# Splitting weights into two parts ahead of their phase and keeping the parts in DRAM

## The chip, the core and the metric

The kernel runs on one core of a Trainium2 chip. The metric is device microseconds of one execution. The engines are named as in the profile: PE (TensorE, with PEld for its weight loads), DVE (VectorE), ACT (ScalarE), POOL (GpSimd) and SP (SyncE, which here only issues DMAs). Each engine works through its own instructions strictly in order; semaphores order the engines against each other. A DMA issued on an engine stands in that engine's order, so an issue that must wait holds up whatever is behind it.

## The reference

Two transformer blocks run one after the other on 2048 tokens of width 1024, all in float32. Cut to what matters:

```
# block 1: gated linear attention (GLA), 4 heads, chunks of 64 tokens
h = rmsnorm(x, g) * (1 + scale) + shift
q, k, v, g_lr, r = split(h @ w_in)
o = chunked_gla(q, k, v, log_sigmoid(g_lr @ w_alpha + b) / 16)
x = rmsnorm(x + gate * ((rmsnorm(o) * silu(r)) @ w_out), final_g)
# block 2: three mixers side by side on one projection
h2 = rmsnorm(x, g_pre) * (1 + scale2) + shift2
p = h2 @ w_in2
y_m = mlstm(p) * silu(mz)            # 4 heads of 96, chunks of 64
y_a = sliding_window(p) * silu(az)   # "swa": 6 heads, 2 kv heads, window 128
y_s = stick_breaking(p) * silu(sz)   # "stick": 4 heads of 64
out = x + gate2 * rmsnorm(concat(y_m, y_a, y_s) @ w_out2, g_post)
```

## The kernel before, in words

**Tiles and phases.** Tokens go in 8 tiles of 256. Six phases follow one another: the GLA phase (two passes over the 8 tiles, head pair p=0 and then p=1, so 16 tiles), out1 (the output projection of block 1, weights `w_out1`), swa (`d_w`), mlstm (`e_wv`, `e_w`), stick (`c_w`) and out2 (`w_out2`). Intermediate tensors (`hT`, `oT`, `h2T`, `yT`) lie in DRAM.

**Precision.** A float32 operand is used as a high part rounded to fp32r and a low part, the rest. `dense3_steps` makes each dense product from three matmuls, high by high (L280), low by high (L281) and high by low (L282). So every weight must be split once.

**Weights.** A phase holds four weight units, `u0` to `u3` (GLA also `wr0`, `wr1`), each as a high and a low tile of [128, 8, 256] (`u0h`, `u0l`), with one buffer per name. A unit of the next phase may therefore be written only after the last matmul of this phase that reads the old one. `weights` (L153) fetches a unit in pieces of 128x512 floats (256 KB) into tiles called `stage`, of which two exist, and splits each piece as it comes: odd pieces with a Copy on ACT (L174) and a subtraction on POOL (L175), even pieces with a scaling on POOL (L150) and a subtraction on DVE (L151). The DMAs are issued on SP (L168).

**Order.** `pipeline` (L180) runs the tiles of a phase. While tile t is mixed (attention or recurrence), `interleave` (L27) takes in turns steps of that mix and steps of the gate of tile t and the dense products of tile t+1. In the last tile of a phase the loads and splits of the next phase's units are emitted there. The emitted program then goes through a scheduler that orders the instructions of each engine by a simulated timeline and by priorities (`high_priority` in `ahead`). So the final order on an engine isn't the emitted one, and it is fixed when the program is built.

**Names used below.** `la`, `E`, `sil`, `vh`, `osq` belong to a GLA tile (`la` is written once per tile on ACT, L584; `bm` on POOL, L592; `vh` on ACT, L549; S0/S1 are the state). `vf` (ACT, L998) is written once per swa tile; L1103 is swa's division of probabilities on POOL. `hn` (POOL, L1396), `nu`, `wsR`, `lfR`, `rows` and `bc` belong to mlstm: gates are written to `rows` in DRAM (L1154, L1160) and read back broadcast as `bc` (L1269), both on SP. `xr` (L786) is the normalised output of block 1, which PE transposes (L364). `ke`, `be`, `aT`, `po` belong to stick.

Of the kernel before, what the change touches and what calls it, by code (L numbers as in the profile page):

```python
# [21 lines left out]
NT = S // T  # L22
# [1 line left out]
EPS = 1e-6  # L24


def interleave(a, na, b, nb):  # L27

    ia = ib = 0
    while a is not None or b is not None:  # L30
        if b is None or (a is not None and ia * nb <= ib * na):
            if next(a, StopIteration) is StopIteration:
                a = None
            ia += 1
        else:
            if next(b, StopIteration) is StopIteration:
                b = None
            ib += 1


class Bank:
# [27 lines left out]
class K:  # L69

    def __init__(self, tc, I, O, ctx):
        self.tc, self.nc, self.I, self.O, self.ctx = tc, tc.nc, I, O, ctx
        nc = self.nc
        P = self.pool
        self.cp = P("cp", 1)
        self.sp = P("stage", 2)
        self.dp = P("dp", 1, DRAM)
        self.wp = P("w", 1)
        self.hp = P("h", 4)
        self.mmp = P("ps_mm", 2, PSUM)  # L80
        self.nmm = self.nw = 0
# [24 lines left out]
        self.acts = []  # L106
        self.table("natural_log_exp_and_others")
# [45 lines left out]
    def weights(self, src, name, stage=None, pool=None, k0=0, k1=None, more=None):  # L153


        pool = pool or self.wp
        k1, n = k1 or src.shape[1], src.shape[2]
        rows = 2 if n == 256 else 1
        w = n + (more.shape[2] if more is not None else 0)
        hi = pool.tile([128, k1 - k0, w], F32R, name=name + "h", tag=name + "h", bufs=1)  # L160
        lo = pool.tile([128, k1 - k0, w], F32R, name=name + "l", tag=name + "l", bufs=1)
        parts = [(src, 0, n, j, min(j + rows, k1)) for j in range(k0, k1, rows)]
        if more is not None:
            parts.insert(1, (more, n, w, k0, k1))
        for d, c0, c1, j, je in parts:
            shape = [128, je - j, c1 - c0]
            st = stage(shape) if stage else self.sp.tile(shape, F32, name="stage", tag="stage")
# [12 lines left out]
    def pipeline(self, n, load, dense, nd, gate, ng, mix, nm, first, lead=0, nxt=None, pri=0):  # L180

        hs = {0: first[0]}
        out, n0 = [], 0
        if first[1]:
            hs[1] = load(1)
        for i, _ in enumerate(first[1] or dense(0, hs[0])):
            if i == 6 and 1 not in hs:  # L190
                hs[1] = load(1)
        if nxt:
            hload, units, ndense, n0 = nxt

        def both(t):
            W = []
            if t + 1 == n and nxt:
                out.append(hload())
                W += [u() for u in units[:2]]
            yield from gate(t, hs.pop(t))  # L200
            if t + 2 < n:
                with self.tc.high_priority(offset=-30):
                    hs[t + 2] = load(t + 2)
            if t + 1 < n:
                yield from dense(t + 1, hs[t + 1])
            elif nxt:
                W += [u() for u in units[2:]]
                out.append(W)
                out.append(ndense and ndense(0, out[0], W))
                if n0:  # L210
                    yield from islice(out[2], n0)
        for t in range(n):
            gt = ng(t) if callable(ng) else ng
            b, nb, na = both(t), gt + (nd if t + 1 < n else n0), nm(t)
            if not nb:
                list(b)
            for _ in range(gt if t < lead else 0):
                next(b)
            interleave(self.ahead(mix(t), pri), na if nb >= 2 * gt else na // 2, b, nb)
        return out  # L220

    def ahead(self, steps, n):
# [215 lines left out]
    def gla_pass(self):  # L438
        nc, tc, I = self.nc, self.tc, self.I
        gw = I["gla_w"]  # L440
        names = ["u0", "u1", "u2", "u3", "wr0", "wr1"]
        W, ST, st = {}, [None, None], {}

        def unit(p, i, **kw):
            return self.weights(I["gla_wr"][p, i - 4] if i > 3 else gw[p, i], names[i], pool=wr if i > 3 else None,
                                more=None if i else I["gla_wx"], **kw)

        def h_of_x(t, parts):
            for k, h in parts:
                nc.sync.dma_start(self.hT[t][:, k:k + 2, :], h)  # L450
                yield k, h

        with ExitStack() as ctx:
            self.psum(ctx, "gla", mm=2, tr=1, pA=1, po=1, kv=1)
            wr = self.open(ctx, "w_gla", 1)
# [12 lines left out]
            parts = self.make_h(wk, banks, self.G1, None, (("hn", 2), ("hn", 2), ("vh", 3), ("vh", 3)))  # L468
            h0 = self.split_h(h_of_x(0, parts), self.B1)
# [26 lines left out]
            def mix(t):  # L496
# [3 lines left out]
                if 6 < t < 15:  # L500
                    self.late_mod(wk, t - 7)

            return self.pipeline(2 * NT, load, dense, 8, gate, 4, mix, lambda t: 6, (h0, None), pri=100,
                                 nxt=(lambda: self.split_h(self.load_h(self.oT[0], wk, 2, 2, "hn")),
                                      self.units("w_out1"), None, 0))

# [227 lines left out]
    def units(self, key):  # L734

        n = self.I[key].shape[0]
        return [lambda j=j: self.weights(self.I[key][j], f"u{j + 4 - n}") for j in range(n)]

    def halves(self, W):

# [281 lines left out]
    def swa_pass(self, h0, W, first):  # L1022
        nc, I = self.nc, self.I
        with self.swa_ctx as ctx:
# [40 lines left out]
            nxt = self.units("e_w")  # L1065
            nxt.insert(0, self.mlstm_wv)
            self.nxt = self.pipeline(NT, lambda t: self.load_hl(self.h2T[t]), lambda t, h: self.swa_dense(t, h, W), 5,
                                     gate, 3, mix, lambda t: 18, (h0, first), pri=60,
                                     nxt=(lambda: self.load_hl(self.h2T[0]), nxt, self.mlstm_dense, 5))

    def swa_rows(self, wk, n, i, qs, kst, v, bias, sink, y, st):
# [99 lines left out]
    def mlstm_open(self):  # L1171
# [11 lines left out]
        m["hg"], m["sk"] = const("m_hg", [128, 3]), const("m_sk", [128, 3])  # L1183
        for key in ("wq", "wk"):
            m[key] = [one(f"{key}{x}", [128, 6, 96], F32R) for x in "hl"]
            for i in range(2):
                js = slice(3 * i, 3 * i + 3)
                st = self.sp.tile([128, 3, 96], F32, name="stage", tag="stage")
# [6 lines left out]
        m["st"], m["ub"] = {}, {}  # L1195

    def mlstm_wv(self):
        parts = [self.weights(self.I["e_wv"], name, None, pool, k0, k1)
                 for name, pool, k0, k1 in (("u0", None, 0, 5), ("ux", self.m_w1, 5, NK))]
        return [a + b for a, b in zip(*parts)]  # L1200

# [353 lines left out]
```

## Time and profile before

| what | before |
|---|---|
| runs | 2162.48, 2162.74, 2167.41 us; median 2162.74 |
| profiled execution | 2172.11 us; span 2170.4 us |
| granted clock over the span | 0.983 of full speed |
| busy PE / DVE / ACT / POOL | 95% / 62% / 41% / 40% |
| moved over the span | 240.01 MB, 111 GB/s |
| q1 (hardware queue, mostly SP's issues) | 187.17 MB, 28.1% of 16 engines |

The span is the profiled execution from its first to its last instruction. PE is busy for 95% of it, so whatever shortens the time without taking matmuls away must come from the other 5%, about 108 us, or from stretches at a lower clock. The 40 slices of the page show PE at 9 in nearly all slices, with dips at the start and at the borders between phases.

### The profile page before, as it was taken

To read this page: it belongs to the slowest core of one execution; us is meant where nothing else is said; L and a number is where in the kernel's file an instruction comes from. 1 tells how busy PE (TensorE), PEld (TensorE's weight loads), DVE (VectorE), ACT (ScalarE), POOL (GpSimd) and SP (SyncE) were. 2 spreads that over 40 slices of the span, in tenths; PEclk is the share of its full clock that TensorE was granted. 3 is DMA by queue.
4 is the path that set the end of the run, shared out by engine and by line. 5 is a ranking of instruction groups with operands and counts; after the bars stand their busy time and mean duration, and the time that the engine had idled before them with its cause. 6 is when DMAs were issued, how large, how long until landed. Compare 5 with 4: busy or idle time off the path is not lost.

```text
span 2170.4 us, 39224 instructions
## 1 busy us (share of the span) xinstructions
PE 2062.5 (95%) x14912; PEld 1880.4 (87%) x14912; DVE 1354.9 (62%) x2517; ACT 894.8 (41%) x2290; POOL 868.6 (40%) x1362
## 2 busy tenths in 40 slices
PE   6999999899999999979999989999789999889998
PEld 6899999899999878879999889999789998777787
DVE  6755655665666467656555545556447788888843
ACT  3534433333333333345555433533335555544411
POOL 3522334522222356554333423334336555663300
PEclk9999999999999999999999999999989999999999
DMA  9522322432332366663222542333431111222252
GB/s 323 181 78 69 107 83 80 138 101 74 88 86 80 118 232 231 212 223 99 93 93 80 153 83 68 90 107 96 115 115 45 45 45 45 65 68 74 67 186 88
DMA packets 122413, 240.01 MB, mean 111 GB/s; under 512 B 13248, under 2 KB 39782, under 8 KB 122224
## 3 DMA queue, kind: packets, MB, share of 16 engines
q1 hardware_dynamic: 108400, 187.17, 28.1%
q0 software_dynamic: 13824, 50.34, 7.3%
q8 instruction: 117, 1.92, 0.4%
q14 instruction: 72, 0.59, 0.1%
HBM read 178.66 MB, written 58.79 MB: 109 GB/s over the span
## 4 chain that ended last, share of the span: by engine, by line
PE 72%; DMA 8%; POOL 6%; DVE 6%; issue 5%; ACT 2%; SPq 0%; DVEq 0%; POOLq 0%; ACTq 0%
PE mm L280 18%; PE mm L282 18%; PE mm L281 18%; PE po L49 3%; PE aT L951 2%; PE qk L1308 1%; PE z L833 1%; DMA stage<-in_c_w 1%; PE z L834 1%; DVE ke L941 1%; DMA stage<-in_w_out 1%; DMA stage<-in_ada_w 1%; PE pT L1112 1%; DMA bc<-rows 1%; POOL u2l L175 1%
## 5 line engine op out<-in xcount | busy, mean ns | idle before, releaser
L941 DVE TENSOR_TENSOR_SCAN ke<-ke,zero 128x512 f32<-128x512 f32 (+3 forms) x160 | 179.6, 1137 | 19.9 <-POOL ke L936 11.5
L280 PE MATMUL mm<-hh,u1h 128*128 128x256 f32 x640 | 187.1, 292 | 1.3 <-DVE mz L976 1.3
L282 PE MATMUL mm<-hh,u1l 128*128 128x256 f32 x640 | 185.5, 290 | 0.0
L281 PE MATMUL mm<-hl,u1h 128*128 128x256 f32 x640 | 184.9, 289 | 0.0
L280 PE MATMUL mm<-u0h,hh 128*128 128x272 f32 (+2 forms) x464 | 155.2, 334 | 12.8 <-DVE y L1437 4.1
L282 PE MATMUL mm<-u0h,hl 128*128 128x272 f32 (+2 forms) x464 | 154.2, 333 | 0.7 <-DVE hl L265 0.4
L281 PE MATMUL mm<-u0l,hh 128*128 128x272 f32 (+2 forms) x464 | 154.0, 332 | 0.0
L280 PE MATMUL mm<-hh,u2h 128*128 128x256 f32 x512 | 147.6, 288 | 1.1 <-DVE gs L568 1.0
L282 PE MATMUL mm<-hh,u2l 128*128 128x256 f32 x512 | 147.1, 288 | 0.0
L281 PE MATMUL mm<-hl,u2h 128*128 128x256 f32 x512 | 146.4, 286 | 0.0
L280 PEld LDWEIGHTS mm<-hh,u1h 128*128 128x128 f32 x640 | 123.8, 193 | 2.3 <-DVE mz L976 1.5
L280 PE MATMUL mm<-u3h,hh 128*128 128x256 f32 (+1 forms) x384 | 124.3, 324 | 0.9 <-DVE vl L550 0.8
L282 PEld LDWEIGHTS mm<-hh,u1l 128*128 128x128 f32 x640 | 123.8, 193 | 0.6 <-issue 0.2
L281 PEld LDWEIGHTS mm<-hl,u1h 128*128 128x128 f32 x640 | 123.7, 193 | 0.5
L282 PE MATMUL mm<-u3h,hl 128*128 128x256 f32 (+1 forms) x384 | 123.3, 321 | 0.0
L281 PE MATMUL mm<-u3l,hh 128*128 128x256 f32 (+1 forms) x384 | 122.5, 319 | 0.0
L280 PE MATMUL mm<-hh,u3h 128*128 128x256 f32 x384 | 111.5, 290 | 4.6 <-ACT sv L864 2.7
L137 ACT ACTIVATE be<-z 128x512 f32<-128x512 f32 (+3 forms) x160 | 86.6, 541 | 69.2 <-PE aT L951 69.0
L282 PE MATMUL mm<-hh,u3l 128*128 128x256 f32 x384 | 111.1, 289 | 0.2 <-DVE mprev L1194 0.2
L281 PE MATMUL mm<-hl,u3h 128*128 128x256 f32 x384 | 111.2, 290 | 0.0
L280 PEld LDWEIGHTS mm<-u0h,hh 128*128 128x128 f32 x464 | 89.1, 192 | 20.7 <-DVE y L1437 4.8
L137 ACT ACTIVATE ke<-z 128x512 f32<-128x512 f32 (+3 forms) x160 | 86.5, 543 | 47.1 <-PE z L834 17.6
(419 smaller groups left out, 6933.8 us busy)
## 6 DMA issues: line engine op xcount, KB each, us to landing
hh<-h2Th POOLq DMA_DIRECT2D x48, 512.0 KB, 6.7
hl<-h2Tl POOLq DMA_DIRECT2D x48, 512.0 KB, 5.8
mvw<-in_mod_w SPq DMA_DIRECT2D x48, 256.0 KB
stage<-in_ada_w SPq DMA_DIRECT2D x32, 256.0 KB
xt<-in_x SPq DMA_DIRECT2D x16, 512.0 KB
stage<-in_gla_w SPq DMA_DIRECT2D x32, 256.0 KB
oT<-oT SPq DMA_DIRECT2D x32, 256.0 KB
hf<-hT SPq DMA_DIRECT2D x32, 256.0 KB
```

The source lines that it names most:

```text
L49: i = self.k.nc.tensor.matmul(out, a, b, start=first is None, stop=stop, skip_group_check=True).ins
L137: i = self.nc.scalar.activation(out, src, func, **kw).ins
L175: self.nc.gpsimd.tensor_tensor(y, st, x.bitcast(F32), op=OP.subtract)
L280: mm(out, ah[k][:, ca], bh[k][:, cb], start=(k == 0), stop=False)
L281: mm(out, ah[k][:, ca], bl[k][:, cb], start=False, stop=False)
L282: mm(out, al[k][:, ca], bh[k][:, cb], start=False, stop=(k == NK - 1))
L833: mm(out, qs[:, h, qt], ks, start=True, stop=False)
L834: mm(out, qs[:, 2 + h, qt], ks, start=False, stop=True)
L941: nc.vector.tensor_tensor_scan(ke[:, 0:w][:, ::-1], ke[:, 0:w][:, ::-1], zero.to_broadcast([128, w]), ke[:, w:w + 1], op0=OP.mult, op1=OP.add)
L951: nc.tensor.transpose(pa[:, j, :], be[:, j * 128:(j + 1) * 128], self.ident)
L1112: nc.tensor.transpose(pt[:, g, :], ss[g][:, kv, sb * 128:(sb + 1) * 128], self.ident)
L1308: mm(p[:, hh, :], w[a][:, idx, :], cu[b][:, blk, :], start=n == 0, stop=n == len(blocks) - 1)
```

## The change

Weights of the first GLA pass are loaded and split as before. All other weights (217 pieces of 128x256 floats, 128 KB, or slightly smaller) go through a generator, `presplit`: a piece is loaded into a tile `wst` (SP, L208), its high part is written into `wsh` by a Copy on ACT (L214) and stored to a DRAM tensor `wd_...h` (SP, L215); the low part is made in place in `wst` by a subtraction on POOL (L216) and stored to `wd_...l` (SP, L217). `wst` and `wsh` have two buffers each. `interleave` calls `tick` after each step, and from the 25th call on each second call emits one step of the generator: in the GLA phase and in the swa phase only. In the GLA phase the loads are ordered behind the last store of `hT` emitted so far (`anchor`), which exists only in the first pass. At the change of phase `ready` loads a unit's parts in four DMAs of 512 KB; nothing is split there any more. `m_wq` and `m_wk` use the same `wst` tiles, in three steps of two heads' columns.

```
+    def presplit(self):
...
+        for p in pieces + [None]:
+            if p:
+                st = self.sp.tile(list(p[0].shape), F32R, name="wst", tag="wst")
+                i = nc.sync.dma_start(st.bitcast(F32), p[0]).ins
+                if self.anchor:
+                    self.behind(i, self.anchor)
+            if old:
+                ot, dst = old
+                hi = self.sp.tile(list(ot.shape), F32R, name="wsh", tag="wsh")
+                nc.scalar.activation(hi, ot.bitcast(F32), AF.Copy)
+                nc.sync.dma_start(dst[0], hi.bitcast(F32))
+                nc.gpsimd.tensor_tensor(ot, ot.bitcast(F32), hi.bitcast(F32), op=OP.subtract)
+                nc.sync.dma_start(dst[1], ot.bitcast(F32))
+            old = p and (st, p[1])
+            yield
+
+    def tick(self):
+        self.nticks += 1
+        if self.nticks > 24 and self.nticks % 2 == 0:
+            next(self.pre, None)
+
+    def ready(self, key, name, pool=None, k0=0, k1=None):
...
+        for a, b in ((k0, m), (m, k1)):
+            for w, d in zip(tiles, self.wd[key]):
+                self.nc.sync.dma_start(w[:, a - k0:b - k0, :].bitcast(F32), d[:, a:b, :].bitcast(F32))
...
-            interleave(self.ahead(mix(t), pri), na if nb >= 2 * gt else na // 2, b, nb)
+            interleave(self.ahead(mix(t), pri), na if nb >= 2 * gt else na // 2, b, nb, self.tick if ticks else lambda: None)
...
         def unit(p, i, **kw):
+            if p:
+                return self.ready(("gla", i), names[i], wr if i > 3 else None)
...
-                nc.sync.dma_start(self.hT[t][:, k:k + 2, :], h)
+                self.anchor = nc.sync.dma_start(self.hT[t][:, k:k + 2, :], h).ins
...
-        return [lambda j=j: self.weights(self.I[key][j], f"u{j + 4 - n}") for j in range(n)]
+        return [lambda j=j: self.ready((key, j), f"u{j + 4 - n}") for j in range(n)]
...
-        parts = [self.weights(self.I["e_wv"], name, None, pool, k0, k1)
+        parts = [self.ready(("e_wv", 0), name, pool, k0, k1)
```

Three places show what the scheduler made of it. The first is ACT in the fourth GLA tile of the second pass, from `la` on (the first row is once per tile). Before:

```order
L584 ACTIVATE la<-mm 128x512
L722 ACTIVATE oT<-tr,gg 128x2x128 x2
L137 ACTIVATE la<-la 128x512
L137 ACTIVATE la<-la,ones 128x512
L137 ACTIVATE eb<-b 128x512
L137 ACTIVATE E_6128<-bm 128x512
L137 ACTIVATE bm<-bm 128x512
L137 ACTIVATE dl<-dl 128x512
L549 ACTIVATE vh<-mm 128x256
L681 ACTIVATE kTh<-tr 128x512
L549 ACTIVATE vh<-mm 128x256
L137 ACTIVATE sil<-mm 128x512
```

Now, in the same tile:

```order
L646 ACTIVATE la<-mm 128x512
L214 ACTIVATE wsh<-wst 128x256
L784 ACTIVATE oT<-tr,gg 128x2x128 x2
L139 ACTIVATE la<-la 128x512
L214 ACTIVATE wsh<-wst 128x256
L139 ACTIVATE la<-la,ones 128x512
L139 ACTIVATE eb<-b 128x512
L214 ACTIVATE wsh<-wst 128x256
L139 ACTIVATE E_6750<-bm 128x512
L214 ACTIVATE wsh<-wst 128x256
L139 ACTIVATE bm<-bm 128x512
L139 ACTIVATE dl<-dl 128x512
```

Copies of pieces (`wsh<-wst`) stand between the instructions of the tile, five of them in these rows. Between this `la` and the next there are 16 of them; in the six tiles t = 3 to 8 there are 10, 9, 12, 10, 12 and 6, and in t = 9 to 13, where no `hT` store holds them back, 13, 15, 16, 17 and 15.

The second place is SP in the swa phase, with the stores of swa's result (`yT<-ya`) of tiles 2 to 6. Before, the stores follow one another until the next phase's weights are fetched:

```order
L1062 DMA yT_106<-ya 128x768
L1062 DMA yT_107<-ya 128x768
L1062 DMA yT_108<-ya 128x768
L1062 DMA yT_109<-ya 128x768
L168 DMA stage<-in_e_wv 128x392 x6
L168 DMA stage<-in_e_w 128x512 x4
L1062 DMA yT_110<-ya 128x768
```

Now, from the store of tile 2 on (the others are apart in the same way):

```order
L1124 DMA yT_106<-ya 128x768
L208 DMA wst<-in_c_w 128x256 x2
L215 DMA wd_c_w1h<-wsh 128x256 x2
L217 DMA wd_c_w1l<-wst 128x256 x2
L208 DMA wst<-in_c_w 128x256 x2
L215 DMA wd_c_w1h<-wsh 128x256 x2
L217 DMA wd_c_w1l<-wst 128x256 x2
L208 DMA wst<-in_c_w 128x256 x2
L215 DMA wd_c_w2h<-wsh 128x256 x2
L217 DMA wd_c_w2l<-wst 128x256 x2
L208 DMA wst<-in_c_w 128x256 x2
L215 DMA wd_c_w2h<-wsh 128x256 x2
```

The pieces go in pairs: two loads, two stores of the high part, two of the low part. A later load, and a result's store, stand behind the pair's stores, which wait for ACT and POOL. Per swa tile 4, 9, 11, 10, 9 and 10 pieces stand there, and 20 more at the end of the phase and beside the first mlstm tile.

The third place is SP at the change from mlstm to stick, where `rows` and `bc` are mlstm's own. Before:

```order
L168 DMA stage<-in_c_w 128x512 x2
L1333 DMA yT_109<-ym 128x768
L168 DMA stage<-in_c_w 128x512 x4
L1154 DMA rows<-lfR 4x256
L1269 DMA bc_17061<-rows 128x4x256
L168 DMA stage<-in_c_w 128x512
L1160 DMA rows<-lfR 4x256
L168 DMA stage<-in_c_w 128x512
L1269 DMA bc_17063<-rows 128x4x256
L168 DMA stage<-in_c_w 128x512 x6
```

Now:

```order
L236 DMA u1h<-wd_c_w1h 128x1024
L236 DMA u1l<-wd_c_w1l 128x1024
L236 DMA u1h<-wd_c_w1h 128x1024
L236 DMA u1l<-wd_c_w1l 128x1024
L1216 DMA rows<-lfR 4x256
L1331 DMA bc_18408<-rows 128x4x256
L236 DMA u2h<-wd_c_w2h 128x1024
L1222 DMA rows<-lfR 4x256
L236 DMA u2l<-wd_c_w2l 128x1024
L236 DMA u2h<-wd_c_w2h 128x1024
L236 DMA u2l<-wd_c_w2l 128x1024
L1331 DMA bc_18410<-rows 128x4x256
```

The pieces through `stage`, whose buffers come free as ACT, POOL and DVE split them, are replaced by loads into the unit itself, and the two `bc` of this place stand behind such loads instead of behind `stage`. On ACT, POOL and DVE the splits of these units are gone from this place.

## Rows read from the trace of the kernel before

**Rows 1.** The page, part 1: PE's busy time.

```profile
PE 2062.5 (95%) x14912; PEld 1880.4 (87%) x14912; DVE 1354.9 (62%) x2517; ACT 894.8 (41%) x2290; POOL 868.6 (40%) x1362
```

**Rows 2.** Windows: stretch, its length, busy by engine, granted clock, DMA share, GB/s.

```profile
350.00:430.00 80.00, 72.90 (x538) 66.85 (x537) 45.48 (x83) 28.20 (x66) 40.87 (x51) 0.98 0.43 129
445.00:715.00 270.00, 270.00 (x2036) 252.50 (x2035) 163.09 (x321) 91.08 (x213) 72.67 (x117) 1.00 0.29 85
720.00:780.00 60.00, 55.06 (x279) 44.21 (x278) 29.85 (x44) 19.38 (x48) 28.24 (x37) 1.00 0.51 170
920.00:980.00 60.00, 49.14 (x339) 46.14 (x338) 34.73 (x55) 23.27 (x54) 34.43 (x55) 0.91 0.66 212
985.00:1180.00 195.00, 195.00 (x1585) 181.92 (x1585) 116.73 (x266) 109.06 (x338) 72.23 (x118) 1.00 0.27 89
1185.00:1300.00 115.00, 102.11 (x717) 95.59 (x716) 58.75 (x123) 48.73 (x138) 39.02 (x53) 0.94 0.46 115
1500.00:1600.00 100.00, 79.43 (x616) 77.08 (x614) 47.87 (x94) 34.43 (x109) 42.50 (x60) 0.88 0.41 120
1860.00:1940.00 80.00, 69.78 (x528) 59.31 (x527) 68.62 (x96) 40.54 (x90) 58.66 (x86) 0.96 0.23 68
```

**Rows 3.** PE's waits, 350 to 450 us: line, releaser, us, times, longest.

```profile
PE tr L719 <- DVE sil L714: 1.6, 1, 1.6
```

**Rows 4.** PE's waits, 720 to 790 us.

```profile
PE po L664 <- POOL S1h L150: 1.6, 1, 1.6
```

**Rows 5.** PE's waits, 920 to 985 us.

```profile
PE tr L364 <- DVE xr L786: 8.6, 1, 8.6
PE mm L280 <- POOL u3h L150: 1.9, 1, 1.9
```

**Rows 6.** DVE's timeline near 944 us: start, us, instruction, idle before and releaser.

```profile
943.77 1.74 DVE L151 TENSOR_TENSOR u1l<-stage,u1h 128x512 fp32r<-128x512 f32 x1 [1.45 <-POOL u1h L150]
945.44 2.46 DVE L786 TENSOR_SCALAR xr<-x,sm 128x1024 f32<-128x1024 f32 x1
```

**Rows 7.** PE's waits, 1500 to 1610 us.

```profile
PE tr L1401 <- POOL hn L1396: 9.8, 2, 5.3
PE nu L1363 <- DVE w L1356: 2.9, 2, 2.1
PE mm L280 <- ACT sv L864: 2.7, 1, 2.7
```

**Rows 8.** ACT's timeline, 1524 to 1531 us.

```profile
1530.82 0.63 ACT L174 ACTIVATE u2h<-stage 128x512 fp32r<-128x512 f32 x1 [6.39 <-DMA stage<-in_c_w]
1531.36 0.19 ACT L137 ACTIVATE sm<-sm 128x4 f32<-128x4 f32 x1
```

**Rows 9.** PE's waits, 1850 to 1945 us.

```profile
PE po L49 <- DVE aT L955: 5.9, 5, 2.5
```

**Rows 10.** Timelines of SP and POOL: issue and first use of one 256 KB load.

```profile
357.84 1.53 SPq L168 DMA_DIRECT2D stage<-in_gla_w  x2
...
360.88 0.62 POOL L150 TENSOR_SCALAR u0h<-stage 128x512 fp32r<-128x512 f32 x1 [1.87 <-DMA stage<-in_gla_w]
```

**Rows 11.** Chain of waits: one store of 4 KB, one of 256 KB.

```profile
1519.54 1.24 DMA rows<-lfR
...
2060.59 2.41 DMA out<-y
```

**Rows 12.** Instructions by line: count, ns min/median/max, first and last start, forms.

```profile
L175 POOL TENSOR_TENSOR u1l<-stage,u1h x14: 1260/1288/2489, 47.8 to 1890.2; 128x512 fp32r<-128x512 f32 x14
...
L998 ACT ACTIVATE vf<-mm x6: 383/384/384, 1012.8 to 1172.5; 128x256 f32<-128x256 f32 x6
...
L1103 POOL TENSOR_TENSOR s<-s,den x42: 609/1040/1054, 995.5 to 1174.4; 128x512 f32<-128x512 f32 x39, 128x256 f32<-128x256 f32 x3
...
L151 DVE TENSOR_TENSOR u1l<-stage,u1h x14: 660/694/1770, 43.8 to 1893.0; 128x512 fp32r<-128x512 f32 x14
```

**Rows 13.** L592, once per GLA tile, between 445 and 725 us.

```profile
L592 POOL TENSOR_TENSOR bm<-b x7: 1061/1062/1066, 456.5 to 717.7; 128x512 f32<-128x512 f32 x7
```

More of the change, by code (lines that the diff above doesn't have):

```diff
@@ L24, with interleave @@
 EPS = 1e-6
-def interleave(a, na, b, nb):
+def interleave(a, na, b, nb, tick):
     ia = ib = 0
@@ L38, in interleave @@
             ib += 1
+        tick()
 class Bank:
@@ L80, in __init__ @@
         self.mmp = P("ps_mm", 2, PSUM)
-        self.nmm = self.nw = 0
+        self.nmm = self.nw = self.nticks = 0
+        self.wd, self.pre, self.anchor = {}, self.presplit(), None
         self.fence = None
@@ L166, in weights @@
             shape = [128, je - j, c1 - c0]
-            st = stage(shape) if stage else self.sp.tile(shape, F32, name="stage", tag="stage")
+            st = stage(shape)
             i = self.nc.sync.dma_start(st, d[:, j:je, :]).ins
@@ L178, in weights @@
         return [hi[:, k, :] for k in range(k1 - k0)], [lo[:, k, :] for k in range(k1 - k0)]
-    def pipeline(self, n, load, dense, nd, gate, ng, mix, nm, first, lead=0, nxt=None, pri=0):
+    def presplit(self):
+        nc, I = self.nc, self.I
+        jobs = [(("gla", i), [(I["gla_w"][1, i], 0)] + ([(I["gla_wx"], 256)] if i == 0 else [])) for i in range(4)]
+        jobs += [(("gla", 4 + i), [(I["gla_wr"][1, i], 0)]) for i in range(2)]
+        jobs += [(("w_out1", i), [(I["w_out1"][i], 0)]) for i in range(4)]
+        jobs += [(("d_w", i), [(I["d_w"][i], 0)]) for i in range(4)]
+        jobs += [(("e_wv", 0), [(I["e_wv"], 0)])] + [(("e_w", i), [(I["e_w"][i], 0)]) for i in range(3)]
+        jobs += [(("c_w", i), [(I["c_w"][i], 0)]) for i in range(4)]
+        jobs += [(("w_out2", i), [(I["w_out2"][i], 0)]) for i in range(4)]
+        pieces = []
+        for key, parts in jobs:
+            K_, w = parts[0][0].shape[1], parts[-1][1] + parts[-1][0].shape[2]
+            d = self.wd[key] = [self.dp.tile([128, K_, w], F32R, name=f"wd_{key[0]}{key[1]}{x}") for x in "hl"]
+            for src, c0 in parts:
+                n = src.shape[2]
+                rows = max(1, min(K_, 256 // n))
+                cols = n // -(-n // 256)
+                for k in range(0, K_, rows):
+                    for c in range(0, n, cols):
+                        ks, cs = slice(k, k + rows), slice(c0 + c, c0 + c + cols)
+                        pieces.append((src[:, ks, c:c + cols], [x[:, ks, cs].bitcast(F32) for x in d]))
+        old = None
+        for p in pieces + [None]:
[13 more added lines that the diff above has]
+            yield
@@ new lines, in tick @@
+    def tick(self):
[3 more added lines that the diff above has]
+    def ready(self, key, name, pool=None, k0=0, k1=None):
+        pool = pool or self.wp
+        out = []
+        k1 = k1 or self.wd[key][0].shape[1]
+        m = (k0 + k1) // 2
+        tiles = [pool.tile([128, k1 - k0, d.shape[2]], F32R, name=name + x, tag=name + x, bufs=1)
+                 for x, d in zip("hl", self.wd[key])]
+        for a, b in ((k0, m), (m, k1)):
+            for w, d in zip(tiles, self.wd[key]):
+                self.nc.sync.dma_start(w[:, a - k0:b - k0, :].bitcast(F32), d[:, a:b, :].bitcast(F32))
+        return [[w[:, k, :] for k in range(k1 - k0)] for w in tiles]
@@ L185, in pipeline @@
+    def pipeline(self, n, load, dense, nd, gate, ng, mix, nm, first, lead=0, nxt=None, pri=0, ticks=False):
         hs = {0: first[0]}
@@ L501, in mix @@
                     self.late_mod(wk, t - 7)
-            return self.pipeline(2 * NT, load, dense, 8, gate, 4, mix, lambda t: 6, (h0, None), pri=100,
+            return self.pipeline(2 * NT, load, dense, 8, gate, 4, mix, lambda t: 6, (h0, None), pri=100, ticks=True,
                                  nxt=(lambda: self.split_h(self.load_h(self.oT[0], wk, 2, 2, "hn")),
@@ L1067, in swa_pass @@
             self.nxt = self.pipeline(NT, lambda t: self.load_hl(self.h2T[t]), lambda t, h: self.swa_dense(t, h, W), 5,
-                                     gate, 3, mix, lambda t: 18, (h0, first), pri=60,
+                                     gate, 3, mix, lambda t: 18, (h0, first), pri=60, ticks=True,
                                      nxt=(lambda: self.load_hl(self.h2T[0]), nxt, self.mlstm_dense, 5))
@@ L1185, in mlstm_open @@
             m[key] = [one(f"{key}{x}", [128, 6, 96], F32R) for x in "hl"]
-            for i in range(2):
-                js = slice(3 * i, 3 * i + 3)
-                st = self.sp.tile([128, 3, 96], F32, name="stage", tag="stage")
+            for i in range(0, 6, 2):
+                js = slice(i, i + 2)
+                st = self.sp.tile([128, 2, 96], F32R, name="wst", tag="wst").bitcast(F32)
                 nc.sync.dma_start(st, I["m_" + key][:, js, :])
```

## The prediction

> **What bounds the kernel now.** I read the page's first part, then a table of windows, then PE's waits in the windows where PE isn't full, then the timelines of the engines that PE waited for there. PE is busy for 2062.5 us of a span of 2170.4 [rows 1], so some 108 us are idle. The windows show where: in the steady GLA tiles (445 to 715 us) and in the steady swa tiles (985 to 1180) PE is busy for the whole stretch at clock 1.00, while around each change of phase it loses time [rows 2]: 7.1 us at the change of GLA pass (350 to 430), 4.9 before out1 (720 to 780), 10.9 before swa (920 to 980), 12.9 before mlstm (1185 to 1300), 20.6 before stick (1500 to 1600) and 10.2 before out2 (1860 to 1940). These 66.6 us are all that the change can win, plus the stretches where the granted clock was below full: .91 before swa, .88 before stick [rows 2]. What it adds, it adds where PE has no idle time at all.
>
> The waits name what PE lost there. At 350 to 450 it is seven waits of 0.3 to 1.6 us on products of DVE, POOL and ACT, the longest for `sil` [rows 3], spread over engines that split weights. Before out1 it waited 1.6 us for POOL's `S1h` [rows 4]. Before swa one wait of 8.6 us was for `xr` of DVE, and one of 1.9 for a split weight [rows 5]; DVE's timeline shows why: a weight subtraction (`u1l`, 1.74 us) that waited for POOL's half stood ahead of `xr`, which itself took 2.46 [rows 6]. Before stick PE waited 9.8 us for `hn`, in two waits of 5.3 and 4.5 us, then 2.9 and 2.7 us for `nu` and `sv` [rows 7]. The first has a plain cause: ACT sat idle for 6.39 us with a Copy of `u2h` whose `stage` piece was late, and the `sm` that `hn` needs stood right behind it [rows 8]. Before out2 PE waits for DVE's `aT` [rows 9] in a window where DVE is busy for 68.62 of 80 us, POOL for 58.66 [rows 2], both with splits among it.
>
> **What goes.** After the first GLA pass no split stands at a border, so I take the waits above that have a split ahead of them. Change of GLA pass: all 7.1, say 7. Out1: 3.0 of the 4.9 (the `S1h` wait of 1.6, the rest splits of the same units; out1's own first tile keeps the other 1.9). Swa: of 8.6 + 1.9 I keep 3.7, because the new order puts the transposes of `xr` behind 44 dense matmuls where 57 stood before, so `xr` still ends last; gain 6.8, and some 2 more if the clock of .91 rises with the gaps gone: 9. Stick: the first `hn` wait of 5.3 goes, and 5.2 of small waits, together 10.5; 2.5 for the clock (79.43 us of matmuls at .88; full clock would give back 9.5, and I take a quarter since half the gaps stay): 13. The second `hn` wait (4.5), `nu` and `sv` are in mlstm's own recurrence and stay. Out2: 8 of 10.2, since 16 pieces' splits go from a window in which POOL and DVE are the wait: half of them cost POOL 1.29 each, half cost POOL .62 and DVE .69 [rows 10, 12], 15 us of POOL and 5.5 of DVE. Sum of gains: 7 + 3 + 9 + 13 + 8 = 40 us. Bounds: 20 (half of each, where another late engine takes a wait's place) to 66.6 plus about 9 for clock.
>
> What is late next at a border is the weight itself: 2 MB a unit instead of 1. The DMA share there is .41 to .66 [rows 2] with 1 MB units; doubling the weights' part leaves room, and each unit waits for its last reader in any case. I cost it at nothing, with 0 to 10 as bounds. SP issues 652 more DMAs; two issues took 1.53 us with their waits [rows 10], and nearly all the new ones stand in stretches where SP has little else, so they count only within the round below. The smaller loads of `m_wq` and `m_wk` lie beside swa and cost nothing; uncovered they would be six DMAs in place of four, some 3 us.
>
> **What is added in the steady tiles.** 217 pieces, each with a load, a Copy on ACT, a subtraction on POOL and two stores. Durations: ACT .38 us by the Copy of the same shape (`vf`) [rows 12]; POOL .65, half of 1.29 for twice the width [rows 12]. 217 of them are 83 us on ACT and 141 on POOL, in stretches where ACT is busy for 34 to 56% and POOL for 27 to 37% [rows 2]. That fits by busy time. What need not fit is the order. Two `wst` and two `wsh` buffers mean that a pair of pieces must be loaded, copied, subtracted and stored before the next pair's load may write; and since SP, ACT and POOL run their instructions in the built order, a late piece holds up the tile's own `la`, `bm` and `hf` loads behind it. So a tile takes at least (pieces / 2) x P, with P the time of one pair's round.
>
> P from rows: a 256 KB load took 3.04 us from issue to first use [rows 10], a 4 KB store 1.24 and a 256 KB store 2.41 [rows 11]. Half way between, 128 KB load in 2.1 and store in 1.8. 2.1 + .38 + .65 + 1.8 = 4.9; .3 for semaphores and SP's issue makes 5.2. To this .3 because POOL's subtraction reached 2.49 us where it met others (median 1.29) [rows 12], and .4 for pieces that arrive while ACT or POOL is in an instruction of its own (.5 to 1 us). P = 5.9 us. Bounds: 3.8 with both DMAs near the 4 KB row, 7.5 with both at the 256 KB rows and the same .7 on top.
>
> A GLA tile takes 43.5 us (six steps from 456.5 to 717.7) [rows 13]; a swa tile 31.9 (five steps from 1012.8 to 1172.5) [rows 12]. In GLA tiles 3 to 8 there are at most 12 pieces: 6 x 5.9 = 35.4, they fit. In tiles 9 to 13 there are 13, 15, 16, 17 and 15: at 5.9 the last four need 44.3, 47.2, 50.2 and 44.3, an excess of .8 + 3.7 + 6.7 + .8 = 12 us. At P = 5.1 it is nothing, at 6.2 21, at 6.7 37, at 7.5 68. In swa, with at most 11 pieces, it is 1 at 5.9, 8 at 6.7, 24 at 7.5. Beside this single pieces delay swa's chain, where POOL's division of 1.04 us [rows 12] feeds the transposes: of 53 pieces one in five with its .65 us unhidden is 7 us (bounds 0 and 34, all of them). Before mlstm, where the last 20 pieces, 8 MB of ready weights and mlstm's first `rows` and `bc` share SP, I take +4 on top of the waits there (bounds 0 and 10).
>
> The Trainium skill, "DMA: Bandwidth & Descriptors", section "Anatomy of one DMA — SWDGE (gpsimd) path", puts a DMA at about 2.0 us fixed and the rest by bytes; I estimate from it 2.3 us for 128 KB, for a load as for a store. By it P would be .7 longer, 6.6, the GLA excess some 34 us instead of 12 and the sum about +12, rival (a) below. The 4 KB store in 1.24 us speaks for a smaller fixed part [rows 11], so I stay at the rows' value.
>
> POOL and DVE collide as well: DVE's `u1l` subtraction ranged from 660 to 1770 ns [rows 12]. The Trainium skill, "SBUF — State Buffer", tells of a shared port pair that GpSimd and VectorE lock against each other, so that the second waits. The ranges agree; it is in the .3 above, and by a full lock each piece would delay DVE by up to .65 us, which DVE's idle 40% takes in GLA [rows 2].
>
> **The sum.** -40 + 12 + 1 + 7 + 4 = -16 us. From the profiled execution's 2172.1 us that is 2156. That execution is 9.4 us over the median of the runs, 2162.74; the same difference from the median gives 2147 us.
>
> **Rivals.** (a) The pair's round throttles. With P at 6.4 or more, the excess in GLA tiles 9 to 13 and in swa eats the gain: at 6.7 it is 37 + 8 + 7 + 4 - 40 = +16, at 7.5 it is 68 + 24 + 7 + 4 - 40 = +63, so 2179 to 2226 us. For it: PE has no slack in these stretches, four tiles stand over the limit at 5.9 already, and a pair's order leaves two buffers no room. Against: the DMAs have .27 to .29 of their share in use there [rows 2], and 4 KB in 1.24 us. It decides from P = 6.4 on, where the sum is zero. Chance .30.
>
> (b) Nothing much. The waits at the borders are taken by what was second there (`nu`, `sv`, `xr`, late 2 MB units), so the gain is 20 instead of 40, against the same 24 of additions: +4; with gain 25 it is -1. 2157 to 2168 us. For it: small waits of several engines in the first window, and the order of the transposes in out1's end. Against: the 6.39 us of ACT [rows 8], whose cause is removed. Chance .14.
>
> (c) The round fits. P at 5.1 or less: -40 + 0 + 0 + 3 + 0 = -37, and with the clock back to 1.00 in the windows before swa and stick up to 8 more: 2118 to 2126. For it: the busy shares; against: queueing behind the tile's own instructions. Chance .16.
>
> My forecast, a gain of 8 to 30 us (2133 to 2155), has .40.
>
> **How the numbers follow.** A measurement of this kernel can't tell less than about .3%, 6.5 us, from no change. Faster: the forecast's .40 and (c)'s .16, .56. Same: (b), .14. Slower: (a), .30. The range: 2118 takes in (c); at the top I go into (a) up to P of about 7, 2195, beyond which about .1 is left. The forecast's own range is 2133 to 2155.
>
> **What would show it.** Right: no weight splits at the borders from 350 us on, the ACT gap before `sm` gone, and PE's waits at 350 to 430 and before out2 under 3 us each. In GLA's second pass, PE waits of some 12 us in all, with ACT, POOL or SP waiting for `wst` loads or stores, and tiles 9 to 13 longer than 43.5 us; in swa short waits for `s` or `pT`. Wrong: tiles 9 to 13 at 50 us or more (then (a)), or at 43.5 with no waits (then (c)), or border waits of the old length under other names (then (b)).

## The result, and the profile after

The changed kernel takes 2286.75 us (median of 4 runs, 2283.67 to 2289.78) against 2165.07 for the kernel before: a ratio of 1.0559 (95% interval 1.0543 to 1.0574). It is 122 us slower; 16 us faster was forecast. The profiled execution took 2289.44 us, 117.3 more than before's.

The page of the kernel after, part 1 and two groups of part 5 (busy us, mean ns, then the idle time before them and what ended most of it); the first line answers to [rows 1]:

```profile
PE 2103.0 (92%) x14912; PEld 1912.5 (84%) x14912; DVE 1295.4 (57%) x2464; ACT 933.7 (41%) x2453; POOL 920.2 (40%) x1472
...
L216 POOL TENSOR_TENSOR wst<-wst,wsh 128x256 fp32r<-128x256 f32 (+2 forms) x217 | 159.6, 741 | 375.2 <-ACT wsh L214 338.5
L214 ACT ACTIVATE wsh<-wst 128x256 fp32r<-128x256 f32 (+2 forms) x217 | 88.3, 411 | 415.3 <-DMA wst<-in_w_out 99.1
```

The pieces' work is small (88 us on ACT, 160 on POOL), but ACT stood idle for 415 us with a Copy next in its order, and POOL for 375 with a subtraction next. Not all of that is loss, since both engines also had idle time before the change.

Windows of the kernel after, in the order and with the columns of [rows 2], each moved to the same place in the program:

```profile
394.00:474.00 80.00, 74.43 (x527) 68.37 (x526) 35.87 (x70) 30.14 (x75) 27.12 (x43) 0.96 0.83 275
495.00:770.00 275.00, 235.12 (x1610) 215.58 (x1609) 130.94 (x262) 93.51 (x242) 108.09 (x166) 0.93 0.55 165
820.00:880.00 60.00, 58.67 (x321) 49.47 (x321) 26.05 (x39) 16.27 (x41) 18.56 (x25) 1.00 0.60 206
1007.00:1067.00 60.00, 59.07 (x403) 54.51 (x402) 29.97 (x46) 24.81 (x62) 24.03 (x36) 1.00 0.95 349
1072.00:1310.00 238.00, 208.91 (x1589) 191.97 (x1587) 114.04 (x271) 126.17 (x393) 109.22 (x174) 0.94 0.54 170
1316.00:1446.00 130.00, 113.93 (x791) 107.83 (x790) 53.13 (x126) 50.26 (x147) 40.99 (x58) 0.91 0.54 163
1628.00:1728.00 100.00, 86.72 (x668) 85.00 (x667) 40.11 (x94) 34.09 (x115) 30.49 (x49) 0.88 0.51 170
1978.00:2058.00 80.00, 74.76 (x616) 64.87 (x616) 67.99 (x93) 40.84 (x91) 43.49 (x84) 0.98 0.42 134
```

Five of the six borders got better: PE's idle time fell from 7.1 to 5.6 us at the change of GLA pass, from 4.9 to 1.3 before out1, from 10.9 to 0.9 before swa, from 20.6 to 13.3 before stick, from 10.2 to 5.2 before out2. Before mlstm, where the last pieces lie, it rose from 12.9 to 16.1. The steady stretches, full before, now have holes: 39.9 us in 495 to 770, 29.1 in 1072 to 1310, and a granted clock of .93 and .94 in place of 1.00. In 495 to 770 PE's 1610 matmuls took 146 ns each, against 133 in the stretch before. From these rows the lower clock is worth some 22 us there (an estimate), beside the 39.9 us of holes.

When a marked instruction first starts, in us of the span, and how much later that is than before (in brackets), worked out from the traces; r1_ready, r6_ahead and r12_wide are experiments below:

| mark | before | after | r1_ready | r6_ahead | r12_wide |
|---|---|---|---|---|---|
| `bm`, GLA tile 3 | 198.9 | 210.1 (+11) | 203.7 (+5) | 201.2 (+2) | 197.8 (-1) |
| `bm`, tile 7 | 368.4 | 412.6 (+44) | 369.2 (+1) | 386.4 (+18) | 370.0 (+2) |
| `bm`, tile 9 | 456.5 | 505.3 (+49) | 453.3 (-3) | 477.6 (+21) | 455.7 (-1) |
| `bm`, tile 14 | 669.9 | 773.5 (+104) | 666.6 (-3) | 704.5 (+35) | 672.5 (+3) |
| last `xr` of out1 | 956.4 | 1040.7 (+84) | 932.7 (-24) | 985.4 (+29) | 948.8 (-8) |
| last `vf` of swa | 1172.5 | 1303.3 (+131) | 1151.8 (-21) | 1240.4 (+68) | 1168.2 (-4) |
| first `hn` of mlstm | 1275.1 | 1421.5 (+146) | 1250.7 (-24) | 1356.7 (+82) | 1268.8 (-6) |
| last `hn` of mlstm | 1578.4 | 1706.0 (+128) | 1530.5 (-48) | 1641.6 (+63) | 1563.0 (-15) |
| end | 2170.4 | 2287.7 (+117) | 2112.6 (-58) | 2223.1 (+53) | 2159.0 (-11) |

The columns are single profiled executions, and before's was 9.4 us over the median of its runs, so a gain read from a mark can be that much too large: r1_ready ends 58 us earlier by the marks, and 48 by the medians.

Nearly all of the loss lies where pieces are made, and it begins in the first pass: 33 us between tiles 3 and 7 with 44 pieces, 55 between 9 and 14 with 68, 44 in swa (from its second tile on) with 53. That is .75 to .84 us a piece in each of the three stretches. Tiles 9 to 13 took 53.6 us each, over the 50 that the prediction had named as the sign of rival (a).

What is waited for in the second pass: PE, then ACT, in 495 to 775 us:

```profile
PE tr L781 <- DVE sil L776: 11.8, 4, 3.5
PE pA L730 <- DVE bm L684: 8.0, 3, 3.8
PE tr L577 <- ACT oT L784: 6.9, 3, 3.4
...
ACT wsh L214 <- DMA wst<-in_d_w: 56.5, 22, 6.3
ACT wsh L214 <- DMA wst<-in_e_w: 27.6, 9, 6.8
ACT wsh L214 <- DMA wst<-in_e_wv: 23.9, 8, 5.7
```

PE waits for the tile's own products (`sil`, `bm`, `oT`), while ACT, which makes or feeds them, stands on pieces not yet loaded, for 108 us in these three rows. One piece on SP and ACT (start, us, instruction, idle before and its releaser):

```profile
512.18 0.42 SPq L208 DMA_DIRECT2D wst<-in_w_out  x1
512.70 0.40 SPq L366 DMA_DIRECT2D mvw<-in_mod_w  x1
513.15 0.42 SPq L217 DMA_DIRECT2D wd_w_out13l<-wst  x1
514.19 0.33 SPq L366 DMA_DIRECT2D mvw<-in_mod_w  x1
515.46 0.33 SPq L215 DMA_DIRECT2D wd_w_out13h<-wsh  x1
516.24 0.33 SPq L208 DMA_DIRECT2D wst<-in_w_out  x1
516.62 0.46 SPq L217 DMA_DIRECT2D wd_w_out13l<-wst  x1
517.19 0.36 SPq L366 DMA_DIRECT2D mvw<-in_mod_w  x1
520.17 0.33 SPq L208 DMA_DIRECT2D wst<-in_w_out  x1
```

```profile
515.02 0.42 ACT L214 ACTIVATE wsh<-wst 128x256 fp32r<-128x256 f32 x1 [2.96 <-issue]
515.34 0.58 ACT L743 ACTIVATE kTh<-tr 128x512 fp32r<-128x512 f32 x1
515.82 0.38 ACT L611 ACTIVATE vh<-mm 128x256 fp32r<-128x256 f32 x1
519.86 0.42 ACT L214 ACTIVATE wsh<-wst 128x256 fp32r<-128x256 f32 x1 [3.67 <-DMA mvw<-in_mod_w]
```

Load at 512.18, Copy at 515.02: 2.84 us. ACT had then been idle for 2.96 us, with `kTh` and `vh` of the tile behind the Copy. (The view names no releaser for this Copy, and a load of `mvw` for the next; that the piece's own load ended the wait is read from the order.) The low part is stored at 516.62, and the next load into that buffer goes out at 520.17. Matched in order for 78 pieces between 450 and 735 us, 69 of whose Copies found ACT already idle, the means are 2.84 from load to Copy, .41 + .16 for the Copy and the gap, .74 + .31 for the subtraction and the gap, and 2.77 from the low part's store to the next load of its buffer: a round of 7.23 us. In swa it is 8.58, in the first pass 9.72.

### The profile page after: what moved, and what is told of

It is laid out like the page before. It is cut to its first block, busy times and chain, and to the rows that moved or that the text cites. A ratio compares the mean times of both kernels' runs of the same rounds, so it can differ in the third digit from the quotient of the medians.

```text
span 2287.7 us, 40779 instructions
## 1 busy us (share of the span) xinstructions
PE 2103.0 (92%) x14912; PEld 1912.5 (84%) x14912; DVE 1295.4 (57%) x2464; ACT 933.7 (41%) x2453; POOL 920.2 (40%) x1472
## 4 chain that ended last, share of the span: by engine, by line
PE 48%; DMA 28%; DVE 8%; issue 5%; POOL 5%; ACT 4%; SPq 1%; POOLq 0%; ACTq 0%; DVEq 0%
PE mm L340 12%; PE mm L342 12%; PE mm L341 12%; DMA wst<-in_w_out 3%; PE po L50 3%; PE aT L1013 2%; POOL wst L216 2%; DMA wst<-in_gla_w 2%; ACT wsh L214 2%; DMA wst<-in_d_w 2%; DMA wst<-in_c_w 2%; DVE ke L1003 1%; PE qk L1370 1%; DMA hf<-in_xT 1%; PE z L895 1%
## 5 line engine op out<-in xcount | busy, mean ns | idle before, releaser
L216 POOL TENSOR_TENSOR wst<-wst,wsh 128x256 fp32r<-128x256 f32 (+2 forms) x217 | 159.6, 741 | 375.2 <-ACT wsh L214 338.5
L214 ACT ACTIVATE wsh<-wst 128x256 fp32r<-128x256 f32 (+2 forms) x217 | 88.3, 411 | 415.3 <-DMA wst<-in_w_out 99.1
L342 PE MATMUL mm<-hh,u1l 128*128 128x256 f32 x640 | 190.1, 297 | 0.0
```

Source lines behind the costliest of these rows:

```text
L214: nc.scalar.activation(hi, ot.bitcast(F32), AF.Copy)
L216: nc.gpsimd.tensor_tensor(ot, ot.bitcast(F32), hi.bitcast(F32), op=OP.subtract)
L342: mm(out, al[k][:, ca], bh[k][:, cb], start=False, stop=(k == NK - 1))
```

## The experiments

Theory A: a piece's round takes longer than the built order gives it, and the engines, each in order, stand on the late piece with the tile's work behind it. Its rivals: B, the work of Copy and subtraction; C and T, the traffic; S, SP alone, which holds the tile's loads behind waiting stores. Ratios are to the kernel before on the same chip, with 95% intervals. That kernel took 2165 to 2170 us on these chips, so where a run is compared with r1_ready from another chip, each is first taken against its own kernel before.

**r1_ready** leaves out all pieces; the units are filled from one small constant.

```
-            if p:
+            if False:
...
+                d = self.cw[:, 0:d.shape[1] * n].rearrange("p (k n) -> p k n", n=n)
```

> The second half of the change alone: every later phase loads its units ready from DRAM (2 MB a unit, no split), and the 217 pieces are left out; all units hold one small constant instead of their weights. Theory A (the round trip of a piece's DMAs, kept in order on SP, ACT and POOL, costs the time) and theory B (the pieces' work on ACT and POOL costs it): both expect only the gains at the borders, which the two traces give as 7 + 4 + 16 + 19 + 11 = 57 us, so about 2108 us (2095 to 2125). Theory C (the doubled loads of units and the DMA traffic cost it): 2150 or more.

Measured: 2116.61 us, .9774 (.9752 to .9797), 48 less than before and 170 less than the changed kernel. The ready units do what they should; the pieces cost 170 us, .78 each.

**r2_engines** adds the Copy and the subtraction of each piece on a resident tile.

```
+                c = nc.scalar.activation(hi, src, AF.Copy).ins
+                self.behind(c, self.lastmm)
+                nc.gpsimd.tensor_tensor(st, src, hi.bitcast(F32), op=OP.subtract)
```

> As r1_ready, plus a Copy on ACT and a subtraction on POOL for each of the 217 pieces, on a resident tile, with no load and no store (constant weights as before). A: the work alone fits beside the tiles, at most 15 us over r1_ready. B: most of the 170 us that the pieces cost comes back, over 2220 us. C: as r1_ready.

Measured: 2120.06, .979 (.9769 to .9811): 3.5 us over r1_ready. B falls. The Copies are ordered behind the dense matmuls here, 49 of them between tiles 9 and 14, not 68 as in the changed kernel; so this weighs the work, not the tighter packing.

**r4_nostore** keeps load, Copy and subtraction.

```
-                nc.sync.dma_start(dst[0], hi.bitcast(F32))
...
-                nc.sync.dma_start(dst[1], ot.bitcast(F32))
```

> As r1_ready, plus load, Copy and subtraction of each piece, but neither of its stores (constant weights as before). A piece's round from load to the next load of its buffer is then 2.8 + .4 + .2 + .7 = 4.2 us instead of 7.2. A: the cost of the pieces falls to about half, some 60 to 100 us over r1_ready, since the order is packed more densely as well. B: 170 over r1_ready. C (two thirds of the pieces' traffic gone): a third of 170, some 55.

Measured: 2174.26, 1.0045 (1.0029 to 1.0062): 58 over r1_ready. The load alone, waited for on ACT, makes a third of the cost, just under A's 60; it is C's number too, so this run doesn't part them.

**r5_paced** is the changed kernel whole, with pieces kept at the ticks' spacing.

```
+                self.behind(i, self.lastmm)
...
+                c = nc.scalar.activation(hi, ot.bitcast(F32), AF.Copy).ins
+                self.behind(c, self.acts[-1])
```

> The changed kernel whole, with all its work and all its DMAs, but a piece's load is ordered behind the last dense matmul emitted before it, and its Copy behind the last activation emitted before it, so that pieces keep the spacing of the ticks: 10 pieces in a GLA tile instead of up to 17, a round of 8 to 9 us between loads of one buffer instead of 5.1. A: the loss in GLA (some 99 us) nearly goes, that in swa (44 us, spacing 6.4 us a round, below 7.2) stays for half or more: 2170 to 2205 us. B and C: no change, 2275 or more.

Measured: 2257.93, 1.0424 (1.0407 to 1.0442): only 29 us better. Spacing alone wasn't enough: the Copies still stood where the load had not landed, against A's forecast. ACT's waits in 455 to 735 us:

```profile
ACT wsh L215 <- DMA wst<-in_d_w: 55.9, 18, 5.4
ACT wsh L215 <- DMA wst<-in_w_out: 31.7, 11, 6.3
```

**r3_dma** has all DMAs, no Copy and no subtraction (the stores write the unsplit piece, the units are constant).

```
-                nc.scalar.activation(hi, ot.bitcast(F32), AF.Copy)
-                nc.gpsimd.tensor_tensor(ot, ot.bitcast(F32), hi.bitcast(F32), op=OP.subtract)
```

> As r1_ready (ready units of one constant), plus the load and both stores of each of the 217 pieces, without the Copy on ACT and the subtraction on POOL; the stores write the unsplit piece. So all the traffic is there and SP's order of waiting loads and stores too, but ACT and POOL have nothing to wait for. A (ACT and POOL, held in order by late pieces, hold up the tile behind them): at most 25 us over r1_ready's 2117. C' (the traffic, or SP held by stores so that the tile's own loads come late): 80 us or more over it, as most of the 170.

Measured: 2228.69, 1.0285 (1.0264 to 1.0306): 111 over r1_ready. A, as I had put it (ACT and POOL alone stand), is wrong: SP stands too. Waits in 455 to 720 us:

```profile
DVE mvacc L375 <- DMA mvw<-in_mod_w: 47.6, 28, 8.4
...
POOL hh L329 <- DMA hf<-hT: 38.8, 6, 11.5
...
PE tr L643 <- DVE gs L637: 18.5, 4, 6.1
```

In the kernel before, in the same window, where PE waited for nothing:

```profile
POOL hh L264 <- DMA hf<-hT: 15.2, 9, 3.5
DVE mvacc L310 <- DMA mvw<-in_mod_w: 14.7, 23, 1.3
```

Here the tile's own loads (`mvw`, `hf`) come late, DVE and POOL wait for them, and PE for DVE.

**r7_waits** and **r8_nowaits** part SP's standing from the traffic: same DMAs at the same places, paced; in r8 the stores read a constant tile, so no store waits for a load.

```
-                    i = nc.sync.dma_start(d, ot.bitcast(F32)).ins
+                    i = nc.sync.dma_start(d, one[...].bitcast(F32)).ins
```

> As r3_dma (ready units of one constant; each piece loaded and stored twice, unsplit, without Copy and subtraction), but loads and stores are ordered behind the last dense matmul emitted, 10 pieces a GLA tile. A store waits for its load, and a load for the stores of the piece two before it. Theory S (SP, standing on a waiting load or store, holds the tile's own loads of hf and mvw behind it): 60 to 110 us over r1_ready's 2117. Theory T (the traffic slows every transfer): the same.

> As r7_waits, with the same number, size and place of DMAs, but the stores read one constant tile instead of the loaded piece, and the loaded piece is read by nobody: no store waits for a load, and no load for a store. S: at most 25 us over r1_ready's 2117. T: as r7_waits, 60 us or more over it.

Measured: r7 2192.03, 1.0097 (1.0060 to 1.0135), some 70 over r1_ready; r8 2156.09, .9923 (.9896 to .9951), some 34 over it. So about half of that cost (36 us) is SP standing on its own DMAs, and half stays without such waits: more than S allowed, less than T. Whether that rest is the traffic or the 651 more issues on SP (.33 us and more each in the timeline above) isn't told apart.

**r6_ahead** is the changed kernel whole, loading two steps ahead: three buffers for the piece and one for the high part, in the space of two and two.

```
-                st = self.sp.tile(list(p[0].shape), F32R, name="wst", tag="wst")
+                st = pool.tile(list(p[0].shape), F32R, name="wst", tag="wst", bufs=3)
...
+            if len(q) > 2 or not p:
+                hi = pool.tile(list(ot.shape), F32R, name="wsh", tag="wsh", bufs=1)
```

> The changed kernel whole, paced as r5_paced (load and Copy both ordered behind the last dense matmul emitted), and with three buffers for the loaded piece and one for the high part in the same SBUF: a piece is loaded two steps before its Copy instead of one, some 9 us ahead in GLA and 6 in swa, so the load's 2.8 us should never be waited for on ACT. A: GLA's loss falls under 20 us in all (r5_paced had some 77 at the end of GLA); in swa the single high-part buffer allows a piece each 3.6 us where 3.2 are wanted, so 10 to 40 us stay: 2130 to 2180 us. C': no better than r5_paced, 2240 or more.

Measured: 2220.4, 1.0246 (1.0229 to 1.0263): 66 us better than the changed kernel, though 40 more than hoped for. By the marks it lost 16 us between tiles 3 and 7 with 41 pieces, 13.5 between 9 and 14 with 49 and 36 in swa with 54: .39, .28 and .67 a piece, with all the DMAs and all the work still there. The loads are hardly waited for any more; the single high-part buffer is, on the landing of its store:

```profile
ACT wsh L218 <- DMA wd_d_w0h<-wsh: 16.4, 7, 5.3
ACT wsh L218 <- DMA wd_d_w1h<-wsh: 12.4, 5, 5.2
```

**r10_queues** is r5_paced with the stores issued by the engines that make the parts.

```
-                nc.sync.dma_start(dst[0], hi.bitcast(F32))
+                nc.scalar.dma_start(dst[0], hi.bitcast(F32))
...
-                nc.sync.dma_start(dst[1], ot.bitcast(F32))
+                nc.gpsimd.dma_start(dst[1], ot.bitcast(F32))
```

> The changed kernel whole, paced as r5_paced, with one edit: the store of a high part is issued on ACT right behind its Copy and that of a low part on POOL right behind its subtraction, so on SP only the pieces' loads are left, which wait for their buffer. S (SP, standing on stores that wait for ACT and POOL, holds hf and mvw) had 36 us between r7_waits and r8_nowaits: some 2215 to 2230 against r5_paced's 2258. If the loss is rather ACT and POOL standing on late loads, no change: 2245 to 2270.

Measured: 2252.05, 1.0403 (1.0381 to 1.0424), 6 us less than r5_paced, and the intervals overlap. SP's standing on stores isn't the main part of what the whole kernel loses; ACT's Copies still wait for loads. The edit isn't clean, though: with the issues on it, POOL was busy for 138.1 us of 455 to 720 instead of 104.4, which may hide a part of what SP gained. In swa it lost 12 us instead of 41, but only 38 pieces lay there, and the 36 that slid behind cost mlstm 22, so the places aren't comparable.

**r9_two, r11_t1free, r12_wide, r13_wide3** start from the kernel before and split only some weights ahead, 256 KB a piece in the two old `stage` tiles, one piece in flight. The lines shown are r12_wide's; r9_two has no test of the tile, r11_t1free tests for tiles 6 to 8 and has `% 6 in (0, 3)`, and r13_wide3 adds `w_out2` and lets pieces into swa tile 6 (22) too.

```
+            st = sp.tile(list(src.shape), F32R, name="stage", tag="stage")
+            self.behind(nc.sync.dma_start(st.bitcast(F32), src).ins, self.lastmm)
+            yield
+            hi = sp.tile(list(src.shape), F32R, name="stage", tag="stage")
+            self.behind(nc.scalar.activation(hi, st.bitcast(F32), AF.Copy).ins, self.lastmm)
...
+        if self.t in (6, 7, 8, 15, 22, 23):
+            return
+        if self.nticks > 24 and self.nticks % 8 in (0, 4):
```

> The kernel before, whole, with only the weights of swa and stick split ahead: 32 pieces of 256 KB in the two old stage tiles, one piece in flight at a time, a piece each 8 ticks of the GLA phase, load and Copy behind the last dense matmul, four ticks (about 9 us) apart; all other phases split at their border as before. From r1_ready the gains are 15 us before swa and 23 before stick. A and S (a piece costs when its round is longer than the order gives it; here it has about 18 us): 0 to 16 us for the pieces, 2130 to 2150 us. If a piece costs .8 us of delay for its own sake, 1.6 for one of twice the size: 32 x 1.6 = 51, 2175 to 2185.

Measured: 2191.34, 1.0088 (1.0065 to 1.0112). Between GLA tiles 3 and 7 it lost 0.7 us with 11 pieces and between 9 and 14 1.5 with 12, but 31 between 7 and 9, where its pieces and the next pass's weights shared `stage`.

> As r9_two, but with no piece in GLA tiles 6 to 8, around the change of GLA pass, where in r9_two the pieces and the next pass's weights took turns at the same two stage tiles and 31 us were lost; a piece each 6 ticks elsewhere. If that collision was r9_two's loss and pieces with a wide round cost next to nothing (r9_two: 2 us in the other GLA tiles), it is 10 us or more faster than before: 2145 to 2160 us. If the pieces' cost only moves, 2175 or more.

Measured: 2168.57, 1.0017 (1.0009 to 1.0026). The 31 us are gone (-1), as said; but 10 us came between tiles 3 and 7, with 11 pieces as in r9_two, at three ticks from load to Copy instead of four. Between 9 and 14, at the same three ticks, 15 pieces lost 2.3, so the spacing alone doesn't explain the 10. The collision is shown; the forecast of a gain was wrong.

> As r11_t1free, but a piece of 256 KB each 8 ticks, its Copy four ticks after its load (r9_two's spacing), none in GLA tiles 6 to 8 and 15, and the last pieces of stick's weights in the first swa tiles. If a wide round makes a piece nearly free (r9_two lost 2 us in GLA tiles 3 to 7 and 9 to 14, r11_t1free 12 with 6 and 3 ticks): before's 2165 - 15 (before swa) - 9 (before stick) + 3 to 8 for the pieces, 2145 to 2155 us. If r9_two's cheap tiles were chance: 2165 or more.

Measured: 2160.52, .9970 (.9957 to .9983), a gain of 6 us, short of the forecast of 2145 to 2155. That is .3%, clear of its interval, but no more than the kernel before varies from run to run. It split 9 pieces between tiles 3 and 7 and lost 2.7 us, 11 between 9 and 14 and lost 3.5: .3 us for 256 KB, .15 for 128 KB, where the changed kernel lost .8. (r9_two, at the same spacing, lost .1 for 256 KB; single executions don't tell these apart.) It also moves less at a time: 18 times 128 KB between tiles 3 and 7, against 44, so rate and spacing both differ. Its windows, second pass and border before swa:

```profile
445.00:715.00 270.00, 267.42 (x2015) 250.22 (x2015) 169.57 (x318) 96.06 (x224) 86.28 (x125) 1.00 0.40 121
920.00:980.00 60.00, 57.68 (x410) 53.72 (x408) 28.62 (x49) 23.63 (x58) 22.97 (x45) 1.00 0.95 347
```

and what ACT waited for its pieces in 455 to 690 us:

```profile
ACT stage L199 <- DMA stage<-in_c_w: 4.4, 3, 2.0
ACT stage L199 <- DMA stage<-in_d_w: 2.0, 2, 1.1
```

PE is nearly full again beside the pieces, at clock 1.00, and ACT's waits for pieces are 6 us for 11 of them, in place of more than 100 for 68.

> As r12_wide, with out2's weights split ahead too, their 16 pieces of 256 KB and the last ones of stick's in swa tiles 0 to 6, at the same spacing of 8 ticks (some 10 us in swa; r1_ready gained 10 us before out2). Wide rounds cheap in swa too: 5 to 10 us below r12_wide, 2138 to 2150. If a piece costs in swa, which has less slack than GLA, what it cost in the changed kernel (44 us for 53 of 128 KB, so 1.7 us for one of 256): 22 x 1.7 = 37 us more, 2170 to 2185.

Measured: 2160.25, .9968 (.9955 to .9982), the same as r12_wide. From the last `hn` to the end it gained 7 us, but its swa pieces cost 13, .3 us for 128 KB: less than the .84 there in the changed kernel, not nothing.

## Why the prediction was wrong

**The gains were right.** 40 us were forecast at the borders; r1_ready gives 48, and after's own marks show 15 before swa (9 forecast), 19 in mlstm up to stick (13), 10 from stick on (8), 4 before out1 (3). At the change of GLA pass 7 were forecast; r1_ready gained 9 there, from `bm` of tile 6 (+5.5) to that of tile 9 (-3.3). The 2 MB units, costed at nothing, are in these 48.

**The term of the pieces' round was too small.** P was put at 5.9 us; 7.23 was measured in the second pass. The 2.1 and 1.8 us for the two DMAs, half way between two rows, were 2.84 and 2.77 with what SP adds; the least in that stretch were 2.03 and 1.65, so I had taken the best case for the mean. With 7.2 the prediction's own formula gives 3 + 11 + 14 + 18 + 11 = 57 us of excess for tiles 9 to 13, and 55 were measured there. That is no test of the formula: P was measured from load to load in these same tiles, where one piece follows another, so half the pieces times P comes out near the tiles' length whatever makes it long. The estimate from the Trainium skill, "DMA: Bandwidth & Descriptors", section "Anatomy of one DMA — SWDGE (gpsimd) path", of 2.3 us a DMA and P = 6.6, was nearer to the trace, though it is stated for another issuing path than SP's; I set it aside for the row of a 4 KB store.

**The step that failed is "In GLA tiles 3 to 8 there are at most 12 pieces: 6 x 5.9 = 35.4, they fit".** They did not: 33 us were lost between tiles 3 and 7 with 10 to 14 pieces a tile (11 on average, which at 7.23 would need only 39.8 us), and 44 in swa, where 1 + 7 had been put. The prediction had said itself that a late piece holds up the tile's own instructions, and then priced only a tile's total. The formula asks whether a tile's pieces fit into its length. But the built order puts each Copy at a fixed place among the tile's own instructions, and a piece that is late at its place stops ACT there, whatever room there is later in the tile. So every piece costs, not the excess over a capacity: .75 to .84 us in all three stretches. r2_engines (work without DMAs, 3.5 us) and r6_ahead (all work and DMAs, but loads two steps ahead: 66 us less, 38 less than r5_paced with its like spacing) show that it is the waiting and not the work, and r12_wide (.15 us for 128 KB, at a lower rate) agrees; r3_dma, r7_waits and r8_nowaits show that SP stands as well, and that some 34 us come with the DMAs even without those waits.

**Rival (a) held in sign**, with a chance of .30, and in that the pieces' round is what the engines wait for. But it used the same formula of excess, so its range of 2179 to 2226 left out the first pass and most of swa, and so the 2287 that came. The +4 before mlstm, where its last pieces lie, was 16.

**Open**: how the loss divides between ACT, POOL and SP in the changed kernel itself (the partial kernels' costs don't add, since each has its own built order). Its own trace points to ACT: in 495 to 775 us DVE waited 25.0 us for `mvw` and POOL 9.9 for `hf`, far from r3_dma's 47.6 and 38.8. Open too is why r8_nowaits still costs 34 us, and what part of the first pass's loss comes from ordering the loads behind the store of `hT`, which no run takes away by itself. More buffers than r6_ahead's were not measured.

## What to carry to other kernels

Work moved into a full stretch "beside" it isn't free if something in an engine's order waits on it: ask of each moved DMA where its consumer stands in the order and how long the transfer takes there on average, not whether busy shares leave room. A load wants to be issued well ahead of the instruction that uses it, with a buffer for that time; one large piece in flight with a wide gap (.15 us lost per 128 KB, at less than half the rate) beat two small ones back to back (.8), and loading two steps ahead at the full rate cost about half as much in GLA (.28 to .39). And count the gain first: here it was at most 48 us, and 217 pieces could not cost more than .22 us each.

## What the runs showed of the hardware that I had not expected

A 128 KB load on SP's queue took 2.03 us at the least and 2.84 on average from issue to its Copy, beside a DMA share of .55. And the granted clock fell after PE's waits: it was .93 in the second pass after, 1.00 before and in r12_wide. In the kernel after, PE was busy for 1.43 of the 5 us from 505 on, and in the next 5 us the granted clock was .66, between the levels of 2.4 GHz (1.00) and 1.2 GHz (.50); so again after 555 (1.56 of 5 us, then .66) and after 695 (1.52, then .66). A part of each stretch's loss is therefore the slower matmuls that followed the waits.
